# Stage transitions of a decoder trunk: units interleaved over banks, steps and loads reordered, one DMA price changed

## The chip, the cores and the metric

The kernel runs on one core of a Trainium2 chip, as one launch. The metric is device time in microseconds (us): the median of several executions. The profile is one further execution, recorded by the hardware profiler. The engines are TensorE (PE; its weight loads are listed apart as PEld), VectorE (DVE), ScalarE (ACT), GpSimd (POOL) and SyncE (SP), which issues every DMA here from one queue.

## What is computed

Two decoder layers over 1024 tokens of 1024 features, all in float32, batch 1. Layer 0 mixes with a gated DeltaNet, layer 1 with stick-breaking attention; then both do the same:

```python
h = h + swiglu(rms_norm(h, ln_ffn[i]), ffn_w_in[i], ffn_w_out[i])
h = h + (p[i] @ ple_w_proj[i]) * jax.nn.sigmoid(rms_norm(h, ln_ple[i]) @ ple_w_gate[i])
...
def swiglu(hn, w_in, w_out):
    gu = hn @ w_in
    return (jax.nn.silu(gu[..., :FFN_HIDDEN]) * gu[..., FFN_HIDDEN:]) @ w_out
```

FFN_HIDDEN is 2816, so 22 tiles of 128. The product `p @ ple_w_proj` (256 features in) is the embedding product, the sigmoid's one the embedding gate.

## The kernel before, in words

Features lie on the partitions, tokens along the free dimension in two halves of 512 (`hf` 0 and 1). A matrix product in float32 is made of three passes in the fast form fp32r: every operand is split into a high part (`hi`, a cast on ACT) and a low part (`lo`, a subtraction on DVE or POOL), and `mm3` (L335) does hi x hi, lo x hi, hi x lo into one PSUM bank. A `unit` (L347) is one bank's product over the 8 feature tiles (`k`), 24 matmuls of 128x512, and waits part by part for its moving operand.

The work after the mixer is `tail` (L1251), once per layer:

- the out-projection of half 1, eight units of f, while DVE normalizes the rows (`norm`);
- `hidden` (L1439): the first hidden tile (t = 0) as four whole units, gate (`fg`) and up (`fu`) for half 0, then half 1; then 21 tiles, t = 1 to 21, of gate and up together by seven products (`STEPS`, a Strassen-like scheme) of 12 matmuls each. The seven use combinations of four blocks of the rows: `factors` (L1355) keeps the tiles (hx, x, y), `combine` (L1371) forms the combinations on DVE, with their splits. Steps 0, 4 and 6 use plain blocks of the normalized rows (`made`, L1546), the others need combinations. The four `dn` banks serve these, one each for a, b, c of `BANKS`, kept over several steps;
- `outputs` (L1554): the second FFN product, again in seven steps per block (c 0 to 4, g 0 and 1), with hidden rows Y read back from DRAM (`yD`, 1 MB each, 37 per layer, `slots`, L1579, a ring of ten places that `hidden` used for its combinations) and the residual rows h1 (`load`, L1563);
- `last_hidden` (L1650) for the two hidden tiles that are left over;
- `ple` (L1681): the embedding gate, sixteen units on two `mm` banks, each followed by a sigmoid on ACT.

Weights come over SP into two `raw` buffers (`weights`, L406). For the seven-step products DVE forms sums of two raw tiles (`sums`, L454: sw, raw, s4), then each of the four factors m of a group is split (L436) into one of three `w` slots or the one `e` slot. Names: `f_s` and `d_s` are the weights of `hidden` and of `outputs`, whi/wlo/ehi/elo their parts.

The order of the work on every engine is decided when the program is built, by a planner, `Flow` (L83). It walks PE's order, which `tail` and its like write out as a list, and keeps a modelled clock for every engine (`issued`, L160). Side tasks are spawned with a priority (0 first) and go on when what they wait for is done on the modelled clock; whatever they issue then takes its place in its engine's queue. A bank is taken by `take` (L320) and given back by `give` (L327), where it counts as free `lead` modelled microseconds before it is (9 in the DeltaNet stage and in the tail of layer 0, 0 from the attention on). The DMAs' modelled time (L195) is their bytes at 360 GB/s, whatever their shape. All instructions are recorded at L64. At the very start, PE runs warm-up products of a mask, triR (`warm`, L826); `ple_products` (L588) makes the embedding products of layer 0 in the DeltaNet stage.

## Time and profile before

| | |
|---|---|
| median of 3 runs | 2863.78 us (2858.65 to 2866.68) |
| profiled execution | 2858.41 us, span 2856.7 us |
| busy: PE, PEld | 2776.9 us (97%), 2283.8 us (80%) |
| busy: DVE, ACT, POOL | 2013.3 us (70%), 1274.6 us (45%), 893.9 us (31%) |
| mean granted clock of PE | 0.987 |
| DMA | 395.89 MB, mean 139 GB/s |

The DeltaNet stage takes the first 750 us, the tail of layer 0 ends near 1500, attention near 2065, the tail of layer 1 fills the rest. Tail 1 repeats tail 0 about 1323 us later. In the lists, "out<-in" are tile names, an idle time stands in brackets with what ended it, and a whole share such as 97% is an average over stages with different limits.

### The profile page before, as it was taken

The page shows a single profiled execution, that of the slowest core. Times are in us where ns is not written, and L with a number is a line of the kernel's source. Part 1 is how long each engine was busy: PE and PEld are TensorE (multiplying, and loading weights), DVE is VectorE, ACT ScalarE, POOL GpSimd, SP SyncE. Part 2 cuts the span into 40 slices and gives each one's busy share as a digit, 9 for nine tenths or more (in the row PEclk, how much of TensorE's full clock was granted, in tenths as well). Part 3 has the DMA queues.
Part 4 walks back from the last instruction along what each step waited for, and adds up shares of the span by engine and source line. Part 5 has one row for each costly group of instructions (what it writes and reads, how often), then busy time and mean ns, then how long its engine had stood idle before and what let it go on. Part 6 is the DMA issues. An engine that isn't in the chain of part 4 may idle for free. (4 is left out here: it accounts for less than half of the span.)

```text
span 2856.7 us, 37760 instructions
## 1 busy us (share of the span) xinstructions
PE 2776.9 (97%) x13192; PEld 2283.8 (80%) x13192; DVE 2013.3 (70%) x3847; ACT 1274.6 (45%) x2567; POOL 893.9 (31%) x754
## 2 busy tenths in 40 slices
PE   8899999999999999999999999999999999999999
PEld 7787787888878888878878888787878888878877
DVE  7867777784676655467867888888685655548783
ACT  6646545553444333322344666666453333322231
POOL 0001110110047666634200223221017666645400
PEclk9999999999999999999999999999999999999999
DMA  4412221227624444587332111114523444477622
GB/s 143 133 56 80 65 73 61 68 81 253 211 77 149 157 145 150 199 312 307 144 122 100 49 60 49 60 51 153 178 88 141 154 147 149 155 304 285 254 79 102
DMA packets 165631, 395.89 MB, mean 139 GB/s; under 512 B 34048, under 2 KB 35392, under 8 KB 155968
## 3 DMA queue, kind: packets, MB, share of 16 engines
q1 hardware_dynamic: 165440, 393.48, 38.7%
q8 instruction: 104, 1.70, 0.2%
q14 instruction: 87, 0.71, 0.1%
HBM read 274.29 MB, written 119.11 MB: 138 GB/s over the span
## 5 line engine op out<-in xcount | busy, mean ns | idle before, releaser
L64 PE MATMUL mm<-x,whi 128*128 128x512 f32 x2912 | 966.7, 401 | 20.8 <-DVE x L64 19.3
L64 PEld LDWEIGHTS mm<-x,whi 128*128 128x128 f32 x2912 | 543.0, 190 | 126.7 <-DVE x L64 27.4
L64 PE MATMUL mm<-x,wlo 128*128 128x512 f32 x1456 | 583.9, 401 | 0.0
L64 POOL TENSOR_TENSOR wlo<-raw,whi 128x512 fp32r<-128x512 f32 x248 | 358.5, 1466 | 505.7 <-ACT whi L64 475.4
L64 ACT CAST whi<-raw 128x1024 fp32r<-128x1024 f32 x233 | 245.0, 1052 | 479.3 <-DVE raw L64 280.2
L64 PE MATMUL dn<-x,whi 128*128 128x512 f32 x1392 | 429.1, 389 | 0.0
L64 PEld LDWEIGHTS mm<-x,wlo 128*128 128x128 f32 x1456 | 276.4, 190 | 47.1
L64 PEld LDWEIGHTS dn<-x,whi 128*128 128x128 f32 x1392 | 261.3, 188 | 54.1
L64 PE MATMUL dn<-x,wlo 128*128 128x512 f32 x696 | 271.2, 390 | 2.3 <-POOL wlo L64 2.3
L64 PE MATMUL dn<-hx,whi 128*128 128x512 f32 x864 | 269.6, 393 | 1.1 <-ACT whi L64 0.7
L64 PE MATMUL dn<-x,ehi 128*128 128x512 f32 x688 | 211.9, 389 | 0.1
L64 DVE TENSOR_TENSOR tt<-u,tt 128x512 fp32r<-128x512 f32 x140 | 147.7, 1055 | 76.0 <-ACT tt L64 75.8
L64 DVE TENSOR_TENSOR v<-v,dn 128x512 f32<-128x512 f32 x110 | 75.3, 685 | 167.9 <-PE dn L64 167.7
L64 PEld LDWEIGHTS dn<-hx,whi 128*128 128x128 f32 x864 | 164.3, 190 | 36.6 <-ACT whi L64 1.5
L64 PE MATMUL dn<-hx,wlo 128*128 128x512 f32 x432 | 170.3, 394 | 4.6 <-POOL wlo L64 4.6
L64 DVE TENSOR_TENSOR wlo<-raw,whi 128x512 fp32r<-128x512 f32 x218 | 146.9, 685 | 23.4 <-ACT whi L64 23.2
L64 PEld LDWEIGHTS dn<-x,wlo 128*128 128x128 f32 x696 | 130.7, 188 | 30.0 <-POOL wlo L64 3.1
L64 PEld LDWEIGHTS dn<-x,ehi 128*128 128x128 f32 x688 | 129.1, 188 | 27.3 <-DVE v L64 0.6
L64 DVE TENSOR_TENSOR E<-E,dn 128x512 f32<-128x512 f32 x132 | 90.1, 684 | 71.6 <-PE dn L64 69.4
L64 ACT CAST tt<-u 128x512 fp32r<-128x512 f32 x140 | 85.2, 620 | 110.2 <-DMA yD<-tt 77.8
L64 PE MATMUL dn<-x,elo 128*128 128x512 f32 x344 | 133.8, 389 | 0.0
L64 POOL TENSOR_TENSOR elo<-sw,ehi 128x512 fp32r<-128x512 f32 x86 | 118.6, 1399 | 0.5 <-ACT ehi L64 0.5
(332 smaller groups left out, 5197.5 us busy)
## 6 DMA issues: line engine op xcount, KB each, us to landing
yD<-tt SPq DMA_DIRECT2D x296, 256.0 KB
x<-yD SPq DMA_DIRECT2D x58, 1024.0 KB
raw<-f_s SPq DMA_DIRECT2D x84, 512.0 KB
raw<-d_s SPq DMA_DIRECT2D x40, 512.0 KB
raw<-w_in SPq DMA_DIRECT2D x33, 512.0 KB
hx<-yD SPq DMA_DIRECT2D x16, 1024.0 KB
x<-oD SPq DMA_DIRECT2D x27, 512.0 KB
raw<-g_out SPq DMA_DIRECT2D x16, 512.0 KB
```

What stands on the lines that cost most here:

```text
L64: r = issue(*args, **kw)
```

## The change

It does these things, with the lines of the kernel before:

- L195: the modelled time of a DMA is multiplied by 128 over the length of its contiguous run where that run is shorter than 128 elements (512 bytes).
- `take` gets a second number, `late`; `ple_products` takes its banks with `late` = `lead`, so at the time when they are really free on the modelled clock.
- A new `units` does several units together, part by part. `hidden` uses it for fg and fu (half 0 on the two `mm` banks, half 1 on two `dn` banks), `ple` for its first two units.
- Tile t = 1 takes its steps in the order 0, 4, 6, 1, 2, 3, 5; its step 6 has a bank of its own ("d"), which `gated` adds in a further DVE instruction. The f_s factors of that tile are split in the order 0, 2, 3, 1.
- The low parts of d_s are all on DVE for the first group of a layer, where POOL had six of them.
- `combine` ends after its second combination and leaves the others to `combine_rest`, spawned on its own.
- `load` (second group) waits for the step two later; `slots` lets a Y load go by other steps: the sixth and seventh five steps before use, the later ones 8 steps before use in place of 10.

```diff
...
                 n *= d
+            run = min(x.ap[-1][1] if x.ap[-1][0] == 1 else 1 for x in outs + ins)
+            n *= max(1, P // run)
             self.clock["dma"] = t + 0.475
...
 
-    def take(self, tag):
+    def take(self, tag, late=0.0):
 
         free = self.slots[tag]
-        if not free or free[0] > self.flow.now:
-            yield lambda: free and free[0] <= self.flow.now
+        if not free or free[0] + late > self.flow.now:
+            yield lambda: free and free[0] + late <= self.flow.now
         free.pop(0)
...
 
+    def units(self, pss, ws, x, ready):
+
+        for k in range(NK):
+            for ps, w in zip(pss, ws):
+                yield from self.part(ps, w, x, k, ready)
+
     def part(self, ps, w, x, k, ready):
...
                     yield
-                eng = nc.gpsimd if key[0] == "fs" or key[0] == "ds" and (j == 0 or key[-1] % 2 == 0) else nc.vector
+                eng = nc.gpsimd if key[0] == "fs" or key[0] == "ds" and key[2] > 0 and (j == 0 or key[-1] % 2 == 0) else nc.vector
                 eng.tensor_tensor(lo[:, j : j + m], src[:, j : j + m], hi[:, j : j + m].bitcast(F32), op=ALU.subtract)
...
             nc.vector.tensor_tensor(t4, rr, lr, op=ALU.subtract)
-            yield from split(key + (0,), r[0])
-            flow.spawn(done(), 3)
-            yield from split(key + (1,), t)
-            yield from split(key + (2,), r[1])
-            flow.spawn(done(), 3)
-            yield from split(key + (3,), t4, 4)
+            for m in (0, 2, 3, 1) if key[0] == "fs" and key[2] == 0 else range(4):
+                yield from split(key + (m,), (r[0], t, r[1], t4)[m], 4 if m == 3 else NK)
+                if m % 2 == 0:
+                    flow.spawn(done(), 3)
 
...
             yield lambda: flow.done(("p", layer, hf)) and flow.done(("p", layer, 2 + hf))
-            yield from self.take("mm")
+            yield from self.take("mm", self.lead)
             ps = self.mmtile()
...
         yield from parts(1, t2)
+        self.flow.spawn(self.combine_rest(y, t2, parts), 3)
+
+    def combine_rest(self, y, t2, parts):
+        tt, sub = self.nc.vector.tensor_tensor, ALU.subtract
         yield from parts(2, y[0][0])
...
 
-        def up(ps, g, key, hf):
+        def up(ps, g, key, hf, tag):
             yield
...
             nc.vector.tensor_tensor(g, g, ps, op=ALU.mult)
-            self.give("mm")
+            self.give(tag)
             hid[0, hf] = g
...
             x = self.rows(X["half", hf])
-            g = None
-            for n, w in zip("gu", ws):
-                yield from self.take("mm")
-                ps = self.mmtile()
-                yield from self.unit(ps, w, x, ("n1", layer, hf))
-                if n == "g":
-                    g = self.t(fp, "acc", bufs=2)
-                    flow.spawn(silu(ps, g, ("sg", layer, 0, hf), "mm"), 0)
-                else:
-                    flow.spawn(up(ps, g, ("sg", layer, 0, hf), hf), 0)
+            tag = ("mm", "dn")[hf]
+            yield from self.take(tag)
+            yield from self.take(tag)
+            pss = [self.t(pp, "dn", bufs=4) if hf else self.mmtile() for _ in ws]
+            yield from self.units(pss, ws, x, ("n1", layer, hf))
+            g = self.t(fp, "acc", bufs=2)
+            flow.spawn(silu(pss[0], g, ("sg", layer, 0, hf), tag), 0)
+            flow.spawn(up(pss[1], g, ("sg", layer, 0, hf), hf, tag), 0)
         for n in "gu":
...
                 flow.mark(key + (2,))
+                if "d" in b:
+                    yield from gated(t, s, b["c"], b["d"])
                 return
...
                 yield from times(s[4], s[0], t, 0)
-            elif i == 6:
-                nc.vector.tensor_tensor(s[1], s[1], b["c"], op=ALU.add)
+            elif i == 6 and "d" not in b:
+                yield from gated(t, s, b["c"])
+            flow.mark(key + (i,))
+
+        def gated(t, s, *banks):
+            for b in banks:
+                nc.vector.tensor_tensor(s[1], s[1], b, op=ALU.add)
                 self.give("dn")
                 yield
-                nc.scalar.activation(s[1], s[1], AF.Silu)
-                yield
-                yield from times(s[1], s[3], t, 1)
-            flow.mark(key + (i,))
+            nc.scalar.activation(s[1], s[1], AF.Silu)
+            yield
+            yield from times(s[1], s[3], t, 1)
 
...
             b, s = {}, {}
-            for i, (m, half) in enumerate(STEPS):
+            order = (0, 4, 6, 1, 2, 3, 5) if t == 1 else range(7)
+            for at, i in enumerate(order):
+                m, half = STEPS[i]
                 w = yield from self.w("fs", layer, t - 1, m)
-                n = BANKS[i]
+                n = "d" if t == 1 and i == 6 else BANKS[i]
                 if n not in b:
...
                     b[n] = self.t(pp, "dn", bufs=4)
-                if i in need:
+                if i in need and n != "d":
                     yield lambda: flow.done(("ev", layer, t, need[i]))
...
                     x = X[i][c]
-                    yield from self.mm3(b[n], (w[0][:, 4 * half + k], w[1][:, 4 * half + k]), (x[:, 0, j], x[:, 1, j]), i < 3 and k == 0, i > 3 and k == 3, True)
-                if half == STEPS[-1][1] and m == 3 or i + 1 < 7 and STEPS[i + 1][0] != m:
+                    yield from self.mm3(b[n], (w[0][:, 4 * half + k], w[1][:, 4 * half + k]), (x[:, 0, j], x[:, 1, j]), (i < 3 or n == "d") and k == 0, i > 3 and k == 3, True)
+                if all(STEPS[e][0] != m for e in order[at + 1 :]):
                     self.drop("fs", layer, t - 1, m)
...
                 for i in (1, 2, 4, 5):
-                    yield lambda: flow.done(("step", layer, i) if g else ("xr", layer, 0 if i < 3 else 5))
+                    yield lambda: flow.done(("step", layer, i + 2) if g else ("xr", layer, 0 if i < 3 else 5))
                     if g == 0 and i in (1, 4):
...
             for n in range(37):
-                at = 14 * (n // 7) + n % 7 - 10
                 if n < 7:
                     yield lambda: flow.done(("xr", layer, FREE[n]))
-                else:
-                    yield lambda: flow.done(("step", layer, at))
+                if n > 4:
+                    yield lambda: flow.done(("step", layer, n - 5 if n < 7 else 14 * (n // 7) + n % 7 - 8))
                 if n > 9:
...
         flow.spawn(loads(), 3)
-        for f, hf in order:
+        for at in [order[:2]] + [[o] for o in order[2:]]:
+            hf = at[0][1]
             x = yield from self.tiles(xkey + (hf,))
-            w = yield from self.w(f"pg{layer}", f)
-            yield from self.take("mm")
-            ps = self.mmtile()
-            yield from self.unit(ps, w, x, xkey + (hf,))
-            flow.spawn(put(f, hf, ps), 0)
-            if hf == 1:
-                self.drop(f"pg{layer}", f)
+            ws, pss = [], []
+            for f, _ in at:
+                w = yield from self.w(f"pg{layer}", f)
+                ws.append(w)
+                yield from self.take("mm")
+                pss.append(self.mmtile())
+            yield from self.units(pss, ws, x, xkey + (hf,))
+            for (f, _), ps in zip(at, pss):
+                flow.spawn(put(f, hf, ps), 0)
+                if hf == 1:
+                    self.drop(f"pg{layer}", f)
```

What that does to the queues, at three places. First PE at the start of half 1 in the first hidden tile of layer 0. whi_1769 and wlo_1770 are the parts of fg, whi_1775 and wlo_1776 those of fu (1775, 1776 with other last numbers after), y_1714 and x_1708 the first rows. Before:

```order
L64 MATMUL mm_1796_8030<-y_1714_7547,whi_1769_7799 128x512 x2
L64 MATMUL mm_1796_8030<-y_1714_7547,wlo_1770_7800 128x512
L64 MATMUL mm_1796_8030<-y_1714_7547,whi_1769_7799 128x512 x2
L64 MATMUL mm_1796_8030<-y_1714_7547,wlo_1770_7800 128x512
L64 MATMUL mm_1796_8030<-x_1708_7541,whi_1769_7799 128x512 x2
L64 MATMUL mm_1796_8030<-x_1708_7541,wlo_1770_7800 128x512
```

and now:

```order
L64 MATMUL dn_1799_8049<-y_1714_7558,whi_1769_7810 128x512 x2
L64 MATMUL dn_1799_8049<-y_1714_7558,wlo_1770_7811 128x512
L64 MATMUL dn_1800_8050<-y_1714_7558,whi_1775_7860 128x512 x2
L64 MATMUL dn_1800_8050<-y_1714_7558,wlo_1776_7861 128x512
L64 MATMUL dn_1799_8049<-y_1714_7558,whi_1769_7810 128x512 x2
L64 MATMUL dn_1799_8049<-y_1714_7558,wlo_1770_7811 128x512
L64 MATMUL dn_1800_8050<-y_1714_7558,whi_1775_7860 128x512 x2
L64 MATMUL dn_1800_8050<-y_1714_7558,wlo_1776_7861 128x512
```

One bank took all of its rows from all k, then the other; now two banks take turns on each part. The embedding stage's first two units change from one to the other in the same manner.

Second, SP's queue ahead of the output stage of layer 0, with the loads of Y (hx, x <- yD, in the order Y0, Y1, ...), of d_s and of the residual rows h1D. Before:

```order
L64 DMA hx_1704_7537<-yD0_89 128x2048
L64 DMA hx_1705_7538<-yD0_89 128x2048
L64 DMA x_1710_7543<-yD0_89 128x2048
L64 DMA x_1711_7544<-yD0_89 128x2048
L64 DMA x_1712_7545<-yD0_89 128x2048
L64 DMA x_1713_7546<-yD0_89 128x2048
L64 DMA raw_2370_11305<-d_s 128x1024
L64 DMA x_1706_7539<-yD0_89 128x2048
L64 DMA y_2373_11333<-h1D0_86 128x512 x2
L64 DMA y_2374_11334<-h1D0_86 128x512 x2
L64 DMA raw_2383_11377<-d_s 128x1024
```

and now:

```order
L64 DMA hx_1704_7548<-yD0_89 128x2048
L64 DMA hx_1705_7549<-yD0_89 128x2048
L64 DMA x_1710_7554<-yD0_89 128x2048
L64 DMA x_1711_7555<-yD0_89 128x2048
L64 DMA raw_2368_11304<-d_s 128x1024
L64 DMA x_1712_7556<-yD0_89 128x2048
L64 DMA y_2374_11344<-h1D0_86 128x512 x2
L64 DMA y_2375_11345<-h1D0_86 128x512 x2
L64 DMA raw_2384_11386<-d_s 128x1024
L64 DMA x_1713_7557<-yD0_89 128x2048
L64 DMA x_1706_7550<-yD0_89 128x2048
```

Y0 to Y5 stood ahead of the first of these d_s loads and Y6 ahead of the second; now Y4 follows the first, Y5 and Y6 follow the second, and the third is ahead of Y7 (rows 450 and 451 of that queue).

Third, DVE's queue at the same stage, second to fifth step. The sums sw, raw, s4 prepare the second group of d_s, the others are evictions of banks into the residual rows. Before:

```order
L64 TENSOR_TENSOR hx_2359_11232<-hx_2359_11232,dn_2384_11382 128x512
L64 TENSOR_TENSOR hx_2359_11232<-hx_2359_11232,dn_2386_11391 128x512
L64 TENSOR_TENSOR hx_2360_11233<-hx_2360_11233,mm_2387_11399 128x512
L64 TENSOR_TENSOR hx_2360_11233<-hx_2360_11233,mm_2388_11409 128x512
L64 TENSOR_TENSOR hx_2360_11233<-hx_2360_11233,dn_2384_11382 128x512
L64 TENSOR_TENSOR hx_2360_11233<-hx_2360_11233,dn_2386_11391 128x512
L64 TENSOR_TENSOR y_2373_11333<-y_2373_11333,dn_2377_11355 128x512
L64 TENSOR_TENSOR y_2373_11333<-y_2373_11333,dn_2380_11369 128x512
L64 TENSOR_TENSOR y_2374_11334<-y_2374_11334,dn_2384_11382 128x512
L64 TENSOR_TENSOR sw_2389_11462<-raw_2370_11305,raw_2383_11377 128x512
L64 TENSOR_TENSOR sw_2389_11462<-raw_2370_11305 128x512
```

and now:

```order
L64 TENSOR_TENSOR hx_2360_11245<-hx_2360_11245,dn_2385_11393 128x512
L64 TENSOR_TENSOR hx_2360_11245<-hx_2360_11245,dn_2387_11403 128x512
L64 TENSOR_TENSOR hx_2361_11246<-hx_2361_11246,mm_2388_11411 128x512
L64 TENSOR_TENSOR hx_2361_11246<-hx_2361_11246,mm_2389_11420 128x512
L64 TENSOR_TENSOR hx_2361_11246<-hx_2361_11246,dn_2385_11393 128x512
L64 TENSOR_TENSOR sw_2390_11438<-raw_2368_11304,raw_2384_11386 128x512
L64 TENSOR_TENSOR sw_2390_11438<-raw_2368_11304 128x512
L64 TENSOR_TENSOR hx_2361_11246<-hx_2361_11246,dn_2387_11403 128x512
L64 TENSOR_TENSOR raw_2368_11304<-sw_2390_11438,raw_2368_11304 128x512
```

The first sum follows the fifth eviction; before, it followed the ninth.

## Rows read from the trace of the kernel before

**Rows 1.** The page: span, busy us (share of the span), instructions

```profile
span 2856.7 us, 37760 instructions
...
PE 2776.9 (97%) x13192; PEld 2283.8 (80%) x13192; DVE 2013.3 (70%) x3847; ACT 1274.6 (45%) x2567; POOL 893.9 (31%) x754
```

**Rows 2.** Waits of PE: total us, times, longest us

```profile
PE mm L64 <- DVE x L64: 19.3, 14, 2.7
PE dn L64 <- POOL wlo L64: 6.9, 4, 2.3
PE mm L64 <- ACT ca L64: 5.5, 3, 3.7
PE mm L64 <- DVE triR L64: 4.2, 1, 4.2
...
PE tp L64 <- DMA X<-Xd: 2.7, 3, 1.7
```

**Rows 3.** Windows: length, busy (count) PE PEld DVE ACT POOL, clock, DMA share, GB/s

```profile
1000.00:1200.00 200.00, 200.00 (x884) 165.61 (x883) 109.58 (x143) 75.25 (x104) 131.03 (x95) 1.00 0.42 147
786.00:812.00 26.00, 19.82 (x69) 14.71 (x68) 24.22 (x39) 13.03 (x23) 2.99 (x2) 0.80 0.00 1
1222.00:1270.00 48.00, 44.22 (x186) 35.46 (x185) 33.06 (x48) 13.16 (x17) 20.86 (x15) 0.96 0.74 284
1424.00:1452.00 28.00, 23.55 (x92) 18.05 (x91) 25.34 (x43) 14.90 (x24) 1.01 (x1) 0.82 0.17 58
2112.00:2130.00 18.00, 13.01 (x46) 9.57 (x45) 17.46 (x29) 10.08 (x17) 1.26 (x1) 0.81 0.00 0
2540.00:2585.00 45.00, 41.23 (x167) 32.89 (x166) 27.86 (x40) 9.24 (x12) 17.37 (x12) 0.92 0.78 294
2745.00:2777.00 32.00, 27.56 (x114) 21.51 (x113) 28.41 (x47) 15.57 (x24) 1.66 (x2) 0.84 0.15 50
```

**Rows 4.** Timeline, PE, first hidden tile: start, us, instruction [idle before]

```profile
799.74 0.80 PE L64 MATMUL mm<-x,whi 128*128 128x512 f32 x1 [2.57 <-DVE x L64]
...
800.76 1.06 PE L64 MATMUL mm<-y,whi 128*128 128x512 f32 x2
801.61 0.63 PE L64 MATMUL mm<-y,wlo 128*128 128x512 f32 x1
...
808.58 0.62 PE L64 MATMUL dn<-hx,whi 128*128 128x512 f32 x2
```

**Rows 5.** Timeline of DVE, same stretch

```profile
799.01 0.68 DVE L64 TENSOR_TENSOR x<-E,x 128x512 fp32r<-128x512 f32 x1
...
810.20 2.37 DVE L64 TENSOR_TENSOR y<-u,y 128x512 fp32r<-128x512 f32 x2
```

**Rows 6.** Timeline of POOL, there and at the output stage's start

```profile
808.43 2.99 POOL L64 TENSOR_TENSOR wlo<-raw,whi 128x512 fp32r<-128x512 f32 x2 [24.68 <-ACT whi L64]
...
1228.11 2.95 POOL L64 TENSOR_TENSOR wlo<-raw,whi 128x512 fp32r<-128x512 f32 x2 [14.96 <-ACT whi L64]
```

**Rows 7.** Page groups, POOL's subtraction: busy us, mean ns

```profile
L64 POOL TENSOR_TENSOR wlo<-raw,whi 128x512 fp32r<-128x512 f32 x248 | 358.5, 1466 | 505.7 <-ACT whi L64 475.4
```

**Rows 8.** Timelines of PE and DVE at the embedding stage's start

```profile
1438.97 1.84 PE L64 MATMUL st<-cst,acc 128*128 128x1 f32 x8
...
1442.15 2.08 PE L64 MATMUL st<-cst,rs 128*128 128x128 f32 x8
...
1441.58 1.46 DVE L64 TENSOR_TENSOR x<-v,x 128x512 fp32r<-128x512 f32 x2
```

**Rows 9.** SP's timeline (layer 0) and the chain (layer 1): start, us

```profile
1212.18 0.33 SPq L64 DMA_DIRECT2D raw<-d_s  x1
...
2524.71 14.78 DMA raw<-d_s
```

**Rows 10.** Timeline of ACT at the embedding stage's start

```profile
1445.68 1.28 ACT L64 ACT_TABLE_LOAD   x1
1446.98 0.60 ACT L64 ACTIVATE u<-mm 128x512 f32<-128x512 f32 x1
```


## The prediction

> **What bounds the kernel.** I read the page first, then the waits of TensorE, then windows around its waits, and there the timelines of the engines that feed it. The page shows TensorE busy for 2776.9 of 2856.7 us [rows 1], so there is little to win but what stands between its matmuls. The list of waits names the operands: 19.3 us on the DVE tile x, 6.9 on POOL's wlo, 5.5 on ACT's ca, 4.2 on triR, 2.7 on the transfer X [rows 2]. Waits alone miss the price of the clock, so I take windows and count matmuls. In the even stretch from 1000 to 1200 us, 884 matmuls take 200 us, 0.2262 us each at granted clock 1.00 [rows 3]. Against that rate the six places at which the tail's stages meet lose this (row length less matmuls times 0.2262):
>
> - first hidden tile (called T1 here): 26 - 69 x 0.2262 = 10.4 us in layer 0, 18 - 46 x 0.2262 = 7.6 in layer 1, at mean clocks 0.80 and 0.81;
> - start of the output stage (T2): 48 - 186 x 0.2262 = 5.9, and 45 - 167 x 0.2262 = 7.2;
> - start of the embedding stage (T3): of 92 matmuls 16 are small sums of squares [rows 8]; 28 - 76 x 0.2262 - 16 x 0.06 = 9.8, the 0.06 an estimate (a quarter of 0.2262 for a quarter of the columns); layer 1, with 24 small ones of 114, 10.2.
>
> Together 51 us of 2858.4: that is what the change aims at. Where TensorE waited, its next matmuls start 0.425 us apart (800.76, two, then 801.61) [rows 4]: the clock has gone to its lower level, 1.2 of 2.4 GHz, so a wait costs itself and a stretch at half rate.
>
> **T1, fg and fu interleaved, bank borrowed, order of tile 1.** Half 1 of the normalized rows becomes usable when DVE has written the low parts. The last one runs at 799.01 and ends at 799.7 [rows 5]; TensorE waited 2.57 us for it [rows 4]. Only the fg unit can be computed while the parts arrive; the fu unit follows from 800.76 and ends at 808.58 [rows 4]. In the changed order both units use each part, so after the last part only 5 matmuls are left, 5 x 0.425 = 2.1 us at the lower clock. The last low part moves up by three DVE instructions, about 1.8 us at the 0.6 us at which DVE starts them. So both end near 799.7 - 1.8 + 2.1 = 800.0 instead of 808.6: 8.5 us. What is late next: tile 1 now starts with steps 0, 4, 6, whose factors are those same rows, 3 steps x 12 x 0.2262 = 8.1 us, then step 1 at 808.2 needs the DVE combinations. DVE has no gap in this stretch (24.22 of 26 us busy [rows 3]), and the last combination of step 1 is 18 instructions behind the last low part, 797.9 + 10.9 = 808.8 if nothing slows DVE. So nothing is lost, or up to 3 us if POOL's f_s subtractions do slow it (a pair of DVE instructions took 2.37 us beside them, 1.2 us too long [rows 5, 6]). I take 2 us, so 6.5 in layer 0. The Trainium skill (SBUF — State Buffer, section "SBUF: two separate sides") says that a DVE instruction with two SBUF inputs and a GpSimd instruction that reads SBUF shut each other out for their whole length. By that, three pairs of POOL subtractions in this stretch could put 6 x 1.3 = 7.8 us into DVE's chain and T1 would give about 1; the trace agrees in kind, with 1.2 us lost beside a pair, not 2.6. Layer 1 loses 7.6 in place of 10.4, so I scale to 5. **Sum -11.5**, ends -17 (nearly all 18.0) and -6. The extra bank for step 6 adds one DVE add per layer, 0.68 us in a stretch with spare time later: nothing. The later combinations (prio 3 in a task of their own) let the low parts go first; they are counted in the 1.8.
>
> **T2, weights earlier, Y loads later.** Here TensorE waits for the low parts of the second d_s group: POOL's pair runs from 1228.11 to 1231.06 [rows 6], and the sums before it stand in DVE's queue behind evictions. The changed queue has these sums after the 5th instead of the 9th eviction of the block; evictions come each 6 matmuls, so 4 x 1.36 = 5.4 us earlier, more than the 3 us that are missing. Besides, group 0's low parts go to DVE: six POOL subtractions of 1.466 us per layer [rows 7] become DVE work of 0.68, on an engine with much time there. That by itself would leave 0 of the 5.9 and 7.2 us. The price is in the SP queue: the sixth and seventh Y load (Y5, Y6) now stand behind the d_s load that SP could issue at 1212.18 only [rows 9], since it waits for a raw buffer, perhaps a microsecond sooner with DVE's quicker subtractions. The second group starts near 1228.1 [rows 6], so the stage begins at 1228.1 - 7 x 2.71 = 1209.1, so Y5 is wanted at 1222.7 and Y6 at 1225.4. The landing to go by is the 14.78 us of a d_s load of half a megabyte, in layer 1's same stretch [rows 9], where the DMA share is 0.78 over the window, as it is 0.74 here [rows 3]. Y5 issued at about 1211 lands by that as late as 1226: a wait of up to 3.3 us, and down to none if it lands in 11. I take 1.3 per layer. **Sum -13.1 + 2.6 = -10.5**, ends -13 and -5. Later Y loads are issued 8 instead of 10 steps before use, 21.7 us; the h1 loads of the second group come five steps, 13.6 us, before use instead of seven, and a late one holds an eviction, not TensorE at once. Nothing, while landings stay under these.
>
> **T3, first pair of the embedding units.** The same pattern: the last low parts run at 1441.58 for 1.46 us [rows 8], and then the second unit still has all its 24 matmuls, 5.4 us, to 1450.9. Interleaved, both units end near 1445.4. But there are two mm banks, and the third unit needs the sigmoid of the first: ACT loads its table at 1445.68 for 1.28 us and the sigmoid runs at 1446.98 for 0.60 [rows 10]. So the third unit starts at about 1447.6 instead of 1450.9: 3.3 to 3.5 us per layer. **Sum -7**, ends -4 and -16 (if ACT's table load were to come early too).
>
> **The rest.** The embedding products of layer 0 wait for ACT's ca, 5.5 us in three times [rows 2], because ACT is at other work in between; its order there does not change, so waiting for a really free bank only lets TensorE do other work first: -1, ends 0 and -5. The new price of short runs shuffles the DeltaNet stage; 2.7 us are waited for X [rows 2]: -1, ends -6 and +8 (the upper end an assumption: three times the 2.7 on top). Eleven more warm-up matmuls at the start lie in the 4.2 us in which TensorE waits for triR anyway [rows 2]: nothing, and at most 11 x 0.11 = 1.2.
>
> **Sum** -11.5 - 10.5 - 7 - 2 = -31: the profiled 2858.4 us become 2827.4. That execution is 5.4 below the median of the three runs, 2863.8, so the median becomes **2833 us**. About 0.3% (8.6 us) is what a measurement of this kernel can tell from no change.
>
> **Rivals.**
> - *The clock stays up as well* (0.12). What is left of the waits is so short that no half-rate stretch follows. In the rows, the mean clock is 0.80 to 0.84 in the four windows of T1 and T3, 0.96 and 0.92 in those of T2, where less time is lost, and 1.00 in the even stretch [rows 3]. Then nearly all 51 us go: 2863.8 - 49 = 2815. The Trainium skill (TensorE: Matmul & The Clock Gate, section on HAM oscillation) has the clock fall after idle stretches and come back with steady work, so it expects this if the gaps go.
> - *DVE remains the bound* (0.18). The low parts come no sooner than DVE writes them; what T1 and T3 save returns as waits in tile 1's steps 1 to 3 and at the third embedding unit. For it: DVE is busy 24.22 of 26 and 25.34 of 28 us in these windows [rows 3], and POOL's subtractions stretch it: 2.37 us for two where two of 0.6 stand otherwise [rows 5, 6]. Then T2's 10.5 stay and a third of the 18.5: -17, so 2847. The Trainium skill's rule named at T1 is on this rival's side.
> - *No gain, by the DeltaNet order* (0.06). 0 to 750 us is shuffled throughout; were its waits to grow by 25 to 30 us, ten times those for X [rows 2], the result is 2858 to 2863, the same as before.
> - *Y loads late, slower* (0.03). Sixty Y loads are issued two steps later. The point: a load that needs more than 8 steps, 21.7 us, to land stops TensorE for the excess. To be slower by over 0.3%, 31 + 8.6 us must come back, 0.66 us at each of sixty, thus landings of 22.4 us: 2863.8 + 9 = 2873. For it: 14.78 us for half the bytes at the stage's start [rows 9]; against: even over the windows of the start, the DMA share is 0.74 and 0.78, and 21.7 us is half as long again as that landing.
> - My forecast has 0.61, alone from 2822 to 2843.
>
> **Range and chances.** The low end is the clock's case, 2815; the high end is DVE's case with its T2 at the lower bound, 2852. Faster by over 0.3%: the forecast, the clock's case and nearly all of DVE's, 0.61 + 0.12 + 0.17 = 0.90. Within 0.3%: 0.07. Slower: 0.03.
>
> **What would show it.** Right: no wait for DVE x or y over 1 us between 788 and 800 other than in pairs, tile 1 beginning at about 800 in layer 0; wlo gone from TensorE's waits; the third embedding unit at about 1447 less what was gained before it. Wrong: new waits on DVE x in tile 1, on the transfer x<-yD at the output stage's start, or DeltaNet's end (the first out-projection) later than before by over 5 us.

## The result, and the profile after

| | before | change |
|---|---|---|
| median (four runs each) | 2861.22 us (2857.21 to 2866.68) | 2844.07 us (2840.20 to 2847.26) |
| ratio, 95% interval | | 0.9941 (0.9925 to 0.9957) |
| profiled execution, span | 2858.41 us, 2856.7 us | 2840.20 us, 2838.5 us |
| mean granted clock of PE | 0.987 | 0.994 |

The change is faster by 17 us. The forecast was 2833, a gain of 31; the range (2815 to 2852) holds the result, and the rival in which DVE stays the bound (2847) is nearer to it than the forecast.

The page of the change, with its busy times:

```profile
span 2838.5 us, 37794 instructions
...
PE 2766.3 (97%) x13203; PEld 2274.6 (80%) x13203; DVE 2027.3 (71%) x3861; ACT 1275.9 (45%) x2567; POOL 886.7 (31%) x742
```

Against [rows 1], PE does 11 matmuls more and is busy 10.6 us less. That fits fewer matmuls at half rate: by the trace's record of the granted clock, the lower level stood for 75 us of the span before and for 33 in the change. POOL has 12 instructions less, six low parts in each layer.

The waits of PE in the change (total us, times, longest us):

```profile
PE mm L64 <- DVE x L64: 8.0, 12, 1.4
...
PE dn L64 <- DVE v L64: 4.0, 4, 1.5
PE dn L64 <- POOL wlo L64: 3.4, 2, 2.3
...
PE mm L64 <- ACT ca L64: 3.0, 3, 2.3
PE mm L64 <- ACT u L64: 2.8, 2, 1.5
...
PE st L64 <- DVE acc L64: 2.5, 3, 1.5
PE dn L64 <- ACT v L64: 2.4, 2, 1.2
...
PE mm L64 <- DVE E L64: 2.1, 2, 1.1
```

The wait for x fell from 19.3 to 8.0 us and that for wlo from 6.9 to 3.4 [rows 2]. But four names stand in the list that did not before: v on DVE, v on ACT, u on ACT, E on DVE, 11.3 us together. The first two are evictions that free a bank for tile 1, the third is the sigmoid that the third embedding unit needs, and the last is the eviction that frees the second bank of half 0.

The same stretches in the change (columns as in [rows 3]), for T1, T2 and T3 of layer 0, and then T1 of layer 1:

```profile
768.00:826.00 58.00, 52.85 (x232) 41.20 (x231) 52.48 (x76) 26.82 (x42) 24.68 (x16) 1.00 0.14 50
1213.00:1261.00 48.00, 48.00 (x213) 39.76 (x213) 34.47 (x53) 12.63 (x15) 19.59 (x15) 1.00 0.74 291
...
1414.00:1446.00 32.00, 27.94 (x114) 22.30 (x113) 27.13 (x45) 15.98 (x25) 1.38 (x1) 0.89 0.18 60
2085.00:2141.00 56.00, 51.00 (x217) 39.55 (x216) 51.47 (x74) 27.31 (x42) 23.26 (x15) 0.97 0.13 48
```

At T1 the clock is now 1.00 and 0.97 where it was 0.80 and 0.81, over longer windows [rows 3]. PE is still idle for 5.2 and 5.0 us in them, in several short waits instead of few long ones. T2's start is full: 213 matmuls in 48 us, no idle time.

Where the 18.2 us between the two profiled executions lie is best read between matmuls that are the same in both programs (numbered in PE's order; the change has 11 more at the start). Each length is the difference of two start times in the timeline of PE:

| stretch (us) | layer 0: before, change | layer 1: before, change |
|---|---|---|
| DeltaNet (0), attention (1) | 687.97, 684.13 (-3.8) | 535.12, 535.26 (+0.1) |
| out-projection | 86.11, 88.99 (+2.9) | 53.59, 54.51 (+0.9) |
| first hidden tile | 34.49, 25.87 (-8.6) | 32.53, 26.65 (-5.9) |
| tiles 1 and 2 | 38.20, 43.47 (+5.3) | 38.15, 43.87 (+5.7) |
| tiles 3 to 21 | 361.76, 361.76 (0) | 361.76, 361.76 (0) |
| output stage, start | 61.35, 55.08 (-6.3) | 69.71, 62.11 (-7.6) |
| output stage, middle | 80.01, 81.52 (+1.5) | 99.96, 102.83 (+2.9) |
| embedding, first units | 26.95, 25.80 (-1.2) | 26.52, 20.68 (-5.8) |
| embedding, rest | 58.26, 58.39 (+0.1) | 75.25, 76.85 (+1.6) |

In layer 1 the border between the last two rows lies ahead of the wait for the sigmoid, in layer 0 behind it; so layer 1's wait is in the +1.6.

Four of these must not be read as effects. The DeltaNet stage took 683.8 to 689.3 us in eleven kernels whose instructions there are those of the change, so -3.8 is within its spread. Attention varied in the same way from 535.2 to 539.8, the out-projection from 86.3 to 89.0 in layer 0 and from 53.5 to 55.3 in layer 1, and the embedding's first units of layer 0 stood at 23.60 in most of those kernels, not 25.80. Where an experiment leaves them alone, the other rows mostly repeat within 0.1 us from kernel to kernel. The exceptions: tiles 1 and 2 take 43.4 to 45.1 us in layer 0 and 42.3 to 43.9 in layer 1, the middle of layer 1 takes 102.8 to 104.7 (the change's is the shortest), the embedding's first units of layer 1 and its rest in layer 0 were once or twice longer by 1.6, and the first hidden tile of layer 1 once by 2.9. The record of the granted clock tells all these apart: after the same waits some matmuls run at half rate in one execution and not in another. The change's own profile has such a stretch in tiles 1 and 2 of layer 1 and none in layer 0. Once, the middle of layer 0 was longer by 1.1, by a longer wait for wlo.

**T1.** The timeline of PE in the change, layer 0, from the first hidden tile through tile 1:

```profile
774.99 0.70 PE L64 MATMUL mm<-hx,whi 128*128 128x512 f32 x2 [1.03 <-DVE E L64]
...
798.98 0.62 PE L64 MATMUL dn<-hx,whi 128*128 128x512 f32 x2
...
801.48 0.39 PE L64 MATMUL dn<-hx,wlo 128*128 128x512 f32 x1
803.05 0.73 PE L64 MATMUL dn<-x,ehi 128*128 128x512 f32 x2 [1.19 <-ACT v L64]
...
815.46 0.74 PE L64 MATMUL dn<-x,whi 128*128 128x512 f32 x2 [0.47 <-DVE v L64]
...
820.52 0.74 PE L64 MATMUL dn<-y,ehi 128*128 128x512 f32 x2 [1.54 <-DVE v L64]
```

Tile 1 begins at 798.98 instead of 808.58 [rows 4], about as forecast (800.0); 1.0 us of that comes from the stages ahead. Then it stops five times. Before step 4 PE waits for the bank of step 0; before a part of steps 1 and 3 for a combination; before steps 3 and 5 for DVE's eviction. Counted from start to start less the usual 0.226, these five take 1.35, 0.36, 0.64, 0.38 and 1.71 us, 4.4 together. At 774.99 the second unit of half 0 waits for a bank that the last out-projection unit still holds: one more place that did not exist when the units ran one after the other.

ACT's copy that frees the bank of step 0 comes directly before 803.05, behind a cast in ACT's queue. From the timeline of ACT:

```profile
801.90 0.61 ACT L64 CAST y<-u 128x512 fp32r<-128x512 f32 x1
802.42 0.58 ACT L64 COPY v<-dn 128x512 f32<-128x512 f32 x1
```

In DVE's timeline (same kernel and stretch) the eviction that step 5 waits for stands behind stretched instructions:

```profile
804.09 1.78 DVE L64 TENSOR_TENSOR tt<-E,u 128x512 f32<-128x512 f32 x1
805.80 1.78 DVE L64 TENSOR_TENSOR y<-u,y 128x512 fp32r<-128x512 f32 x1
...
815.32 1.17 DVE L64 TENSOR_TENSOR y<-u,y 128x512 fp32r<-128x512 f32 x1
816.42 1.77 DVE L64 TENSOR_TENSOR x<-E,x 128x512 fp32r<-128x512 f32 x1
818.11 1.76 DVE L64 TENSOR_TENSOR u<-u,tt 128x512 f32<-128x512 f32 x1
819.79 0.68 DVE L64 TENSOR_TENSOR v<-v,dn 128x512 f32<-128x512 f32 x1
```

And POOL's timeline shows what runs beside them, the f_s low parts:

```profile
800.60 3.02 POOL L64 TENSOR_TENSOR wlo<-s,whi 128x512 fp32r<-128x512 f32 x1 [17.67 <-ACT whi L64]
803.59 3.44 POOL L64 TENSOR_TENSOR wlo<-sw,whi 128x512 fp32r<-128x512 f32 x2
...
817.60 3.40 POOL L64 TENSOR_TENSOR wlo<-sw,whi 128x512 fp32r<-128x512 f32 x2
```

**T2.** SP's timeline at the output stage's start (layer 0): the d_s load goes out at 1205.77 instead of 1212.18 [rows 9], and the two Y loads go behind it.

```profile
1205.77 0.33 SPq L64 DMA_DIRECT2D raw<-d_s  x1
1206.15 0.90 SPq L64 DMA_DIRECT2D x<-yD  x2
```

POOL's low parts of the second group then start 9.7 us earlier than the 1228.11 of [rows 6], and in layer 1 a new pair is late, far behind the start (timeline of POOL):

```profile
1218.38 2.55 POOL L64 TENSOR_TENSOR wlo<-raw,whi 128x512 fp32r<-128x512 f32 x2 [10.92 <-ACT whi L64]
...
2636.56 2.96 POOL L64 TENSOR_TENSOR wlo<-raw,whi 128x512 fp32r<-128x512 f32 x2 [12.71 <-ACT whi L64]
```

The stage itself begins 4.3 us earlier (the sum of the table's rows ahead of it), so the net is 5.4 us. The sums ahead of these low parts, in DVE's timeline before:

```profile
1224.30 0.69 DVE L64 TENSOR_TENSOR sw<-raw,raw 128x512 f32<-128x512 f32 x1
```

and in the change:

```profile
1214.54 0.69 DVE L64 TENSOR_TENSOR sw<-raw,raw 128x512 f32<-128x512 f32 x1
```

The trace's DMA completions, matched to the loads in the order of issue, tell when the d_s load that these sums need had landed: at 1222.4 before and at 1212.7 in the change, 1.9 us ahead of the sums in both, and 13.9 and 8.5 us behind the stage's start. No wait for a Y load stands in PE's list, before or now. PE now waits in the middle, here in layer 1:

```profile
2639.57 0.50 PE L64 MATMUL dn<-hx,wlo 128*128 128x512 f32 x1 [2.30 <-POOL wlo L64]
```

**T3.** PE at the embedding stage of the change, layer 0: two parts waited for, then the third unit held by ACT's sigmoid.

```profile
1425.52 0.50 PE L64 MATMUL mm<-x,whi 128*128 128x512 f32 x1 [1.19 <-DVE x L64]
...
1428.59 0.50 PE L64 MATMUL mm<-x,whi 128*128 128x512 f32 x1 [1.41 <-DVE x L64]
...
1440.67 0.73 PE L64 MATMUL mm<-x,whi 128*128 128x512 f32 x2 [1.45 <-ACT u L64]
```

### The profile page after: what moved, and what is told of

The parts are those of the page before. It is cut to its first block, busy times and chain, and to the rows that moved or that the text cites. A ratio compares the mean times of both kernels' runs of the same rounds, so it can differ in the third digit from the quotient of the medians.

```text
span 2838.5 us, 37794 instructions
## 1 busy us (share of the span) xinstructions
PE 2766.3 (97%) x13203; PEld 2274.6 (80%) x13203; DVE 2027.3 (71%) x3861; ACT 1275.9 (45%) x2567; POOL 886.7 (31%) x742
## 5 line engine op out<-in xcount | busy, mean ns | idle before, releaser
L64 PE MATMUL mm<-x,whi 128*128 128x512 f32 x2880 | 955.8, 401 | 12.6 <-DVE x L64 8.0
L64 PE MATMUL dn<-x,whi 128*128 128x512 f32 x1776 | 549.3, 390 | 1.9 <-DVE x L64 0.9
L64 POOL TENSOR_TENSOR wlo<-raw,whi 128x512 fp32r<-128x512 f32 x236 | 345.7, 1485 | 441.0 <-ACT whi L64 414.7
L64 PEld LDWEIGHTS dn<-x,whi 128*128 128x128 f32 x1776 | 333.3, 188 | 73.9 <-DVE x L64 3.3
L64 PE MATMUL dn<-x,wlo 128*128 128x512 f32 x888 | 346.2, 390 | 0.0
L64 PEld LDWEIGHTS dn<-x,wlo 128*128 128x128 f32 x888 | 166.8, 188 | 34.2
L64 POOL TENSOR_TENSOR wlo<-sw,whi 128x512 fp32r<-128x512 f32 x102 | 145.3, 1441 | 2.0 <-ACT whi L64 2.0
L64 POOL TENSOR_TENSOR rs<-ms,nhalf 128x4 f32<-128x4 f32 x11 | 12.3, 1121 | 338.9 <-DVE ms L64 267.4
L64 DVE SCALAR_TENSOR_TENSOR ca<-xe,conv,ca 128x512 f32<-128x512 f32 x144 | 108.4, 755 | 4.3 <-ACT ca L64 3.6
L64 POOL TENSOR_TENSOR t<-t,nhalf 128x4 f32<-128x4 f32 x16 | 18.3, 1141 | 295.3 <-DVE t L64 244.7
```

The lines of the kernel that those rows point to most:

```text
L64: r = issue(*args, **kw)
```

## The experiments

In each, the edit is made on the changed kernel, and the stretches named are those of the table above, with the change's value in brackets. Three questions were open. Why did tiles 1 and 2 take back 5.3 and 5.7 us: because DVE's chain of normalizing, combining and evicting sets the end of tile 1 whatever PE does (theory A), or because the new order of steps and banks makes the waits (theory B)? What made T2's gain, the later Y loads or the low parts moved to DVE? And what are the embedding's pairs and the price of short runs worth? Each was run once, but for the last.

**Units one after the other again, step order kept**

```diff
-            yield from self.take(tag)
-            yield from self.take(tag)
-            ...
-            yield from self.units(pss, ws, x, ("n1", layer, hf))
+            ...
+            for w in ws:
+                yield from self.take(tag)
+                ...
+                yield from self.unit(ps, w, x, ("n1", layer, hf))
```

> The change with one thing undone: gate and up of the first hidden tile are again computed one after the other, in the banks of the change; the step order 0, 4, 6, 1, 2, 3, 5 stays. Span of the change 2838.5 us; there the first hidden tile is 10.0 us (layer 0) and 8.0 us (layer 1) shorter than before, and tile 1 after it 5.4 and 5.6 us longer. Theory A (DVE's chain of combinations, stretched by POOL, sets tile 1, so what is saved before is waited for behind): the first hidden tile grows by 8 to 10 us per layer, tile 1 loses its waits of 4.5 us per layer, net +3 to +5 per layer, span 2845 to 2848. Rival B (the waits in tile 1 come from its step order and banks, not from DVE being late): they stay, net +8 to +10 per layer, span 2855 to 2858.

Measured: first hidden tile 32.57 and 32.70 (25.87, 26.65), tiles 1 and 2 40.20 and 39.28 (43.47, 43.87). Interleaving saves 6.7 and 6.0 us where it stands and gives back 3.3 and 4.6 right after: 5 us over both layers, or 3.3 to 6.5 with the spread of tiles 1 and 2. That is nearer to theory A's picture (3 to 5 per layer) than to B's (8 to 10): PE reaches tile 1 earlier and waits there for what DVE and ACT were going to deliver at that time anyway. About 1 us before step 4 and 0.9 before step 5 stays even so, which A alone does not give.

**Tile 1 in the old order, no extra bank**

```diff
-            order = (0, 4, 6, 1, 2, 3, 5) if t == 1 else range(7)
+            order = range(7)
...
-                n = "d" if t == 1 and i == 6 else BANKS[i]
+                n = BANKS[i]
```

(The f_s factors are split in the order 0, 1, 2, 3 again too.)

> The change with one thing undone: tile 1 takes its steps as 0, 1, 2, ... again, without the extra bank; gate and up stay interleaved. Theory A: step 1 is wanted 2.7 us after the first hidden tile instead of 8.1, its operands are no sooner there, so 5 us more are waited for before step 1 and the waits for evictions go: net +1 to +4 per layer, span 2841 to 2846. Rival B: the waits of 1.35 us (step 4 behind step 0 on one bank) and 1.7 us (step 5) go and nothing comes in their place: -2 to -3 per layer, span 2833 to 2835.

Measured: tiles 1 and 2 44.73 and 43.68 (43.47, 43.87). Neither theory's figure: the new order of the steps and the extra bank are worth nothing that exceeds the spread. The waits only get another name, as PE's timeline of this run shows at step 1 of layer 0:

```profile
802.40 0.39 PE L64 MATMUL dn<-hx,whi 128*128 128x512 f32 x1
805.25 0.79 PE L64 MATMUL dn<-hx,whi 128*128 128x512 f32 x1 [2.46 <-DVE hx L64]
```

In the old order PE needs a combination, hx, before DVE has it; in the new order it waits for banks. Both come from the same two queues.

**The first group's f_s low parts from POOL to DVE**

```diff
-... key[0] == "fs" or key[0] == "ds" ...
+... key[0] == "fs" and key[2] > 0 or key[0] == "ds" ...
```

> The change with one thing altered: the low parts of the f_s weights of tile 1 are subtracted on DVE instead of POOL (5 to 7 subtractions per layer). Theory A with shutting out: beside POOL's five subtractions from 800 to 821 us, DVE instructions of 0.68 us took 1.17 to 1.78, 5.4 us in all; on DVE the five cost 5 x 0.6 = 3.0: tile 1's waits shrink by 1 to 2.5 us per layer, span 2834 to 2837. Rival (the two engines do not hinder each other, the long DVE instructions have another cause): DVE gets 3 to 4 us more work in the stretch that bounds, tile 1 grows by 2 to 4 us per layer, span 2842 to 2846.

Measured: tiles 1 and 2 45.85 (+2.4) and 41.25 (-2.6). Of both, 1.6 us is the clock: this run has the half-rate stretch in layer 0 and not in layer 1, the change's profile the other way round. Like with like it is about +0.8 and -1.0. In layer 0 the wait before step 5 grew:

```profile
820.28 0.82 PE L64 MATMUL dn<-y,ehi 128*128 128x512 f32 x2 [3.82 <-DVE v L64]
```

DVE's timeline shows why: POOL's subtractions for the next group, at 812 to 822, still stretch the combinations ahead of the eviction that step 5 waits for. It runs at 819.55 (819.79 in the change), while PE is ready for it sooner than there.

```profile
813.90 1.77 DVE L64 TENSOR_TENSOR x<-E,x 128x512 fp32r<-128x512 f32 x1
815.59 1.76 DVE L64 TENSOR_TENSOR u<-u,tt 128x512 f32<-128x512 f32 x1
...
819.55 2.72 DVE L64 TENSOR_TENSOR v<-v,dn 128x512 f32<-128x512 f32 x4
```

**The first two groups' f_s low parts on DVE**: the same edit with `key[2] > 1`, again on the change.

> The change with the low parts of the first two f_s groups (tiles 1 and 2) on DVE instead of POOL; with the first group alone, the wait for DVE's eviction ahead of step 5 of tile 1 grew to 4.0 us in layer 0, beside POOL's subtractions for the second group, and shrank to 0.9 in layer 1. If it is POOL's subtractions that stretch DVE (1.77 us for an instruction of 0.68): the DVE instructions of tile 1 all take 0.7 us, tile 1 waits under 2 us in place of 4.4 in both layers, tile 1's stretch 43 to 45 us (46.7 to 48.2 in the change) and 33 to 36 (36.6 to 38.2). Rival: DVE's own load of 14 more subtractions is the price, the wait ahead of step 5 stays 2 to 4 us.

Measured: tiles 1 and 2 41.44 and 42.15 (43.47, 43.87). With POOL idle in this stretch, DVE's instructions are back at their short time, the low parts themselves as well (DVE's timeline):

```profile
804.28 1.28 DVE L64 TENSOR_TENSOR hx<-tt,hx 128x512 fp32r<-128x512 f32 x2
...
815.84 0.68 DVE L64 TENSOR_TENSOR wlo<-raw,whi 128x512 fp32r<-128x512 f32 x1
```

So the stretching is POOL's doing, and it costs 2.0 and 1.7 us of the path; this compares like with like, with the half-rate stretch in layer 1 of both and in layer 0 of neither. The waits did not go, as PE's timeline of this run has it:

```profile
801.93 0.73 PE L64 MATMUL dn<-x,ehi 128*128 128x512 f32 x2 [0.81 <-ACT v L64]
...
817.78 0.73 PE L64 MATMUL dn<-y,ehi 128*128 128x512 f32 x2 [1.75 <-DVE v L64]
```

What is left, 3.3 and 4.0 of the 5.3 and 5.7 us, is put down to the work that DVE and ACT have to do in the stretch, and to the place of the evictions in their queues. That is argued from these waits; no run took such work away or moved an eviction alone.

**Step 6 ahead of step 4, half 0 one unit after the other**

```diff
-            for m in (0, 2, 3, 1) if key[0] == "fs" and key[2] == 0 else range(4):
+            for m in (0, 3, 2, 1) if key[0] == "fs" and key[2] == 0 else range(4):
...
-            order = (0, 4, 6, 1, 2, 3, 5) if t == 1 else range(7)
+            order = (0, 6, 4, 1, 2, 3, 5) if t == 1 else range(7)
```

(With the first run's loop for half 0 alone.)

> The change with two things altered in two separate stretches. Steps of tile 1 in the order 0, 6, 4 instead of 0, 4, 6: if the wait of 1.35 us ahead of step 4 is for the bank that step 0 has just filled (an ACT copy of 0.58 us behind other casts), it goes, -1.3 us per layer in tile 1; if step 4 waited for its weights or rows, it stays or moves to step 6. Half 0 of the first hidden tile one unit after the other, half 1 interleaved: if the wait of 1.2 us at its start is for the second bank, held by the last out-projection, it goes, -1.2 us per layer, and half 1, whose parts come late, is as fast as in the change (17.6 and 16.7 us); rival: half 0's own parts are late too, and the wait comes back inside it.

Measured: span 2846.6, slower by 8. Both waits went: the one before step 4, with step 6 between it and step 0, and the one for the second bank, so that the first hidden tile fell to 24.39 and 25.22 (25.87, 26.65). But tiles 1 and 2 were no shorter for it, 44.89 and 43.44 (43.47, 43.87), and the rest of `hidden` took 6.4 and 5.0 us more, where nothing was edited. From DVE's timeline:

```profile
830.15 0.69 DVE L64 TENSOR_TENSOR sw<-raw,raw 128x512 f32<-128x512 f32 x1 [5.62 <-DMA raw<-f_s]
```

The factors are split in another order, so a raw buffer comes free later and its next load goes out later; the sums of that load stand in DVE's queue ahead of evictions, and PE waits for these (10.5 us on `DVE E`). The last run below, with the same half 0 but the change's order of steps and splits, has none of that. A good edit failed at a third resource.

**Y loads and residual rows as early as before**

```diff
-                    yield lambda: flow.done(("step", layer, i + 2) if g else ...)
+                    yield lambda: flow.done(("step", layer, i) if g else ...)
...
-                if n > 4:
-                    yield lambda: flow.done(("step", layer, n - 5 if n < 7 else 14 * (n // 7) + n % 7 - 8))
+                if n > 6:
+                    yield lambda: flow.done(("step", layer, 14 * (n // 7) + n % 7 - 10))
```

> The change with one thing undone: Y loads and residual loads of the output stage are let go as early as before. Stretches compared, in us (change, before): start of the output stage 13.4 + 28.3 in layer 0 (before 18.2 + 29.8) and 47.4 in layer 1 (before 55.0); its middle 81.5 (80.0) and 102.8 (100.0), where the change has new waits of 1.3 and 2.5 us for wlo. If the later loads are what lets the d_s weights and their sums come earlier: the start goes back to 18.2 + 29.8 and 55.0, the middle to 80.0 and 100.0, net +4.7 per layer. Rival (the start gains by the first group's low parts and the loads alike, either is enough): the start stays at 13.4 + 28.3 and 47.4 and only the new waits go, net -1.5 and -2.9.

Measured: start of the output stage 62.66 and 69.67 (55.08, 62.11; before 61.35, 69.71), middle 80.15 and 99.96, as before the change. The old wait is back (waits of PE):

```profile
PE dn L64 <- POOL wlo L64: 7.0, 4, 2.4
```

The whole gain of T2's start comes from the later loads of Y and of the residual rows, and so do the new waits in the middle. In this run DVE's sums of the second group start at 1223.72, behind nine evictions; in the change at 1214.54. The DMA completions (layer 0) say how. The d_s load that the sums need is issued about as early behind the stage's start (2.0 us here, 1.6 in the change), but lands 14.3 us behind it, against 8.5. In this order Y5 and Y6 stand ahead of it in SP's queue; the loads of Y, 1 MB each, complete 2.5 us apart there, and two of them behind the d_s load in place of ahead account for 5 of these 5.8 us.

**Group 0's d_s low parts back on POOL**

```diff
-key[0] == "ds" and key[2] > 0 and (...)
+key[0] == "ds" and (...)
```

> The change with one thing undone: the low parts of the first d_s group are on POOL again as before (six subtractions per layer); the later Y loads and earlier sums stay. If the start of the output stage gained by the earlier place of the sums in DVE's queue (as the prediction has it): nothing moves, span 2837.5 to 2840. If it gained by the quicker subtractions of the first group: the waits for wlo of 2.3 us and the half-rate stretch come back, +4 to +7 per layer, span 2847 to 2852.

Measured: start 55.08 and 62.11, the change's to the hundredth. These twelve subtractions on DVE are worth nothing there. The span, 2845.0, differs in other stretches, by their spread, DeltaNet (688.89) and attention (538.40) above all.

**One factor's d_s low parts on DVE in every group**, against the new wait in the middle:

```diff
-key[0] == "ds" and key[2] > 0 and (...)
+key[0] == "ds" and key[2] > 0 and key[-1] > 0 and (...)
```

> The change with one thing added: of every d_s group the first factor's low parts are on DVE instead of POOL (two subtractions per group of some 19 us). If the new waits in the middle of the output stage (1.3 us in layer 0, 2.5 in layer 1, for wlo) come from POOL's pair of 2.5 to 3.0 us for that factor: they go, the middle takes 80.0 us instead of 81.5 and 100.0 instead of 102.8 (to 104.7 with a half-rate stretch). Rival (DVE cannot take 1.4 us per group more, evictions come late): waits for DVE E or hx, the output stages longer than in the change.

Measured: middle 83.25 and 102.55 (81.52, 102.83), a miss. POOL has 36 subtractions less, and PE waits for DVE instead (waits of PE):

```profile
PE dn L64 <- DVE wlo L64: 4.4, 6, 1.4
```

**Late first Y loads, early later ones**

```diff
-... n - 5 if n < 7 else 14 * (n // 7) + n % 7 - 8 ...
+... n - 5 if n < 7 else 14 * (n // 7) + n % 7 - 10 ...
```

> The change with half of its rule for Y loads undone: the sixth and seventh Y load and the residual loads stay late, the Y loads from the eighth on are let go 10 steps before use again. If the start of the output stage gains by the first loads alone and the new waits for wlo in its middle come from the later Y loads (their megabytes now fall together with the d_s loads of that group): start 13.4 + 28.3 us in layer 0 and 47.4 in layer 1 as in the change, middle 80.0 and 100.0 instead of 81.5 and 102.8: -1.5 and -2.9 us, no wait for wlo at all. Rival (it is the later ones that make room for the d_s load of the second group): start 18 to 19.4 + 29.8 and 55.0 again, +7 us per layer.

Measured: start 55.15 and 62.18, so the later Y loads from the eighth on have no part in the gain: Y5 and Y6 make it, or the residual rows, whose gate stays the change's. No run parts these two; but the residual rows h1 of the second group follow that d_s load in SP's queue before the change as after it, and Y5 and Y6 changed sides. Middle 81.91 and 100.23 (81.52, 102.83): in layer 1 the new wait is gone, in layer 0 it only moved, from 1320.2 to 1285.3 (PE's timeline):

```profile
1285.31 0.50 PE L64 MATMUL dn<-x,wlo 128*128 128x512 f32 x1 [1.56 <-POOL wlo L64]
```

**Embedding units not interleaved**

```diff
-        for at in [order[:2]] + [[o] for o in order[2:]]:
+        for at in [[o] for o in order]:
```

> The change with one thing undone: the first two units of the embedding stage one after the other again. The stretch of the stage's start takes 25.8 us in layer 0 and 28.5 in layer 1 in the change (27.0 and 34.4 before; 23.6 to 25.8 and 28.5 to 30.1 in the runs that do not touch it). If the interleaving is worth the predicted 3.5 us per layer: 27 to 29 and 33 to 35. Rival (DVE's low parts bound both, the saved time goes to the waits for the sigmoid): within 1 us of the change.

Measured: first units 28.17 and 27.83 (25.80 and mostly 23.60; 20.68), rest of layer 1 75.25 (76.85). Interleaving gives 2.4 to 4.6 us in layer 0 and 7.2 less 1.6 in layer 1, so 8 to 10 together. Alone, each unit waits for the parts (PE's timeline):

```profile
1428.32 0.50 PE L64 MATMUL mm<-x,whi 128*128 128x512 f32 x1 [2.08 <-DVE x L64]
1431.38 0.80 PE L64 MATMUL mm<-x,whi 128*128 128x512 f32 x1 [2.10 <-DVE x L64]
```

**Short runs priced by bytes again**: the line `n *= max(1, P // run)` of the DMA model left out.

> The change with one thing undone: the planner's old price of DMAs with short runs. The DeltaNet stage up to the last product before the out-projection takes 684.1 to 689.3 us in five executions of the change and of kernels with the same queues there, 688.0 before. If the new price helps (predicted 1 us): 689 to 692, and the waits for the transfer X grow. Rival (no effect that stands out of the spread of one queue's executions): 684 to 689.5. If the price hurts: under 683.

Measured: DeltaNet 688.52, inside the 683.8 to 689.3 of the kernels with the new price. No effect is resolved, of either sign, that exceeds this spread. (The eleven matmuls at the start go with the price: 13192 here.) By chance the run tells something of T1, where PE's instructions are the change's: the clock fell in the first hidden tile of layer 1, which took 29.52 us in place of 26.65, and tiles 1 and 2 then took 40.98, where the others take 42.3 to 43.9. Part of what PE loses ahead of tile 1 it need not wait for there.

**The pieces that helped, together**: the two ways of loading Y, half 0 one unit after the other (the wait for its second bank goes), and the f_s low parts of two groups on DVE; step order and split order as in the change.

> A version meant to beat both: the change, with half 0 of the first hidden tile one unit after the other (worth the wait of 1.2 us per layer at its start), the low parts of the first two f_s groups on DVE (tile 1 shorter by 1.7 to 2.0 us per layer) and the Y loads from the eighth on let go 10 steps before use (2.6 us in layer 1, nothing in layer 0, where a wait came elsewhere). If the pieces add up: 2.6 + 2.4 + 3.7 = 8.7 us below the change, which is at 0.9941 of before: ratio 0.991, span of the profile 2827 to 2836. If they take the same time from each other (DVE the common bound in tile 1): only the Y loads and a microsecond or two remain, ratio 0.9925 to 0.994.

Measured five times: 2836.33 us median (2828.55 to 2837.94) against 2861.57 for the kernel before, ratio 0.9907 (0.9892 to 0.9921). The interval does not meet that of the change. First hidden tile 24.30 and 25.52, tiles 1 and 2 42.48 and 41.33, middle of layer 1 100.25: 8.8 us less than in the change's profile, where the pieces came to 8.7; the part in tiles 1 and 2 carries their spread. What PE still waits for in tile 1 (v) and in tile 2 (E), from the waits of PE:

```profile
PE dn L64 <- DVE v L64: 3.3, 2, 1.7
...
PE dn L64 <- DVE E L64: 1.8, 2, 0.9
...
PE dn L64 <- ACT v L64: 1.5, 2, 0.7
```

## Why the prediction was right, and where it was wrong

Right in sign and range; too large by some 13 us of 31. Term by term, between the two profiled executions:

| term | forecast | measured | in other kernels with the same instructions there |
|---|---|---|---|
| T1 (first hidden tile, tiles 1 and 2) | -11.5 | -3.5 | -1.9 to -5.2 (six) |
| T2 (start and middle of the output stage) | -10.5 | -9.5 | -6.9 to -8.0 (six) |
| T3 (embedding) | -7 | -5.3 | -5.0 to -7.5 (eleven) |
| the rest | -2 | +0.1 | |

T1 is the miss whichever execution is taken, and lies outside its bounds (-17 and -6) in all of them. T2 was lucky in the profiled one.

- **T1, the failed step: "So nothing is lost, or up to 3 us ... I take 2 us".** The first half of T1 was right: 8.5 us earlier was forecast for layer 0, and the first hidden tile is 8.6 us shorter; in layer 1 it is 5.9. The second half asked only whether the *combinations* come in time for step 1. They nearly do, with 0.2 us of idle time at 811.25. It did not ask which *banks* are free. Step 4 goes into the bank of step 0, which ACT must first copy out; step 5 waits for an eviction that stands behind combinations on DVE; and half 0 needs two banks at a time at which one is still in use. Only the combinations' queue was priced, not the evictions' in the same queues. 2 us and the layer 1 share of it were forecast, 5.3 and 5.7 measured.
- **The rival "DVE remains the bound"** describes this: the greater part of what T1 saves returns in tile 1. Its terms differ, though. It wanted waits on steps 1 to 3 for x and y; in the change they stand at steps 4 and 5, for banks. In the old order of steps they do stand at step 1 for hx, and cost the same. And T3 did not return its gain, as that rival had it.
- **POOL beside DVE.** A DVE subtraction takes 0.68 us with POOL idle and 1.77 in the middle of POOL's pair; the stretches in tile 1 of layer 0 add 5.4 us to DVE's chain. The Trainium skill (SBUF — State Buffer, section "SBUF: two separate sides") has the two engines shut each other out; the trace and the run with POOL idle agree with it in kind. By that rule T1 was to keep about 1 us in layer 0. It kept 3.3 there: of the 5.4 us that DVE's chain lost, 2.0 were on the path.
- **The clock's rival** had its condition come true in part, and not its time. The clock is 1.00 at T1 and T2 of layer 0 (0.97 at T1 of layer 1, 0.89 at T3), yet PE is idle 5.2 us in T1's window. With shorter waits most half-rate stretches went; the waits themselves stayed, in another place.
- **T2: the sum was nearly right, the mechanism only in part.** The sums come 5.4 us earlier relative to the stage's start (1224.30 to 1214.54, less 4.3), which is the forecast's 5.4, and PE gains by that as forecast. But the forecast had it from their place behind fewer evictions alone. The load that they need had landed only 1.9 us ahead of them, so in the old order of loads no place in DVE's queue could have brought more than that; the landing had to move too, which the forecast did not ask. The later Y loads, entered as a price, 2.6 us for Y5 and Y6, are what moved it: with the early loads back the sums are late again. They were never waited for: in layer 0 they went out at 1206, not at 1211, and landed 9.0 and 11.4 us later, not 14.78. And the low parts on DVE, part of the argument, are worth nothing. In place of the price come 1.5 and 2.9 us in the middle (4.8 in the longest of the other executions of layer 1), which the forecast looked for on the Y loads and which are on POOL's low parts. Why the later loads hurt there was shown only as far as that they do; which of the loads between is late was not tried.
- **T3** was right in its limit: the third unit waits for the sigmoid, in both layers. The forecast of 3.3 to 3.5 per layer came out as 1.0 here in layer 0 (3.2 in most runs) and 4.2 in layer 1. The run without the interleaved pair puts all of it there, and more: it is slower at this place than the kernel before, for which no run gives the cause.
- **The rest.** The wait for ca fell from 5.5 to 3.0 us, but stood at 3.0 to 4.6 in other runs with the same queues, and with the old price at 5.5; DeltaNet's length shows nothing beyond its spread. -2 was neither confirmed nor refuted. The eleven extra matmuls at the start do not lie in the wait for triR, as the forecast has it: they read triR and follow that wait, and the first other product starts at 15.16 us in place of 13.73. What that costs later is not resolved. The out-projection's +2.9 and +0.9 come with waits for acc that are there in some executions only.

## What to carry to other kernels

When work is moved forward on the engine that bounds the time, ask for each step that it now reaches sooner not only for its operands but for its output bank: who empties it, and what stands ahead of that eviction in the queue. A wait that changes its name with the order of the work (hx, then v) while its length stays is a sign that the feeding engines have too much to do in the stretch; here, letting DVE run without POOL beside it paid about 2 us per layer, and reordering paid nothing. And a load gate may be worth more than an engine: two large loads put behind a small urgent one gave the time that the moved subtractions and the place in DVE's queue were credited with. Ask of such a place when its load has landed before moving what uses it.

## What was not expected of the hardware

- DVE's 128x512 fp32 subtraction takes 0.68 us alone and 1.77 between POOL subtractions of 1.7. POOL pays as well, and first: at 800.60 its subtraction took 3.02 us (1.27 to 1.29 alone, at 777 to 780), while the three DVE instructions from 801.20 to 802.40 beside it took 0.68 each; only then came the stretched ones.
- After the same waits, in the same order of instructions, some executions have a stretch at half rate and others not: the embedding's first units of layer 0 take 23.60 or 25.8 us, tiles 1 and 2 of layer 1 42.3 or 43.9. A difference under 2 us in one stretch can be read from single profiles only where the granted clock is the same in both.
- DeltaNet and attention vary by 5.5 and 4.6 us between kernels that have the same instructions there. An edit that aims at a few us in them cannot be judged by one profile.
